# A decoder block's last PSUM banks seeded with a row, its first products split off, and a new list schedule

## The chip, the cores and the metric

The kernel runs on one core of one Trainium2 chip. The metric is the device time of one execution in microseconds. The median of 3 runs of the kernel before is 896.83 us (896.61 to 897.23).

## The reference

One layer of a decoder trunk, for one sequence of 512 positions with 1024 channels, 256 memory tokens, 4 heads, and 2816 channels in the feed-forward part, all in f32:

```python
h = rmsnorm(x, norm_mix_g)
p_a, p_b, q, p_g = split(h @ w_in)                  # 3072, 2048, 1024, 3072 columns
gb, gc, v = split(p_a)
y_a = (gb * causal_conv3(gc * v)) @ w_a_out
u, ug = split(p_b)
y_b = silu(layernorm(causal_conv31(u * sigmoid(ug)) + bias)) @ w_b_out
k, vm = split(rmsnorm(mem, norm_mem_g) @ w_kv)
y_c = attention(q, k, vm) @ w_att_out               # 4 heads, 256 memory tokens
g = sigmoid(p_g + b_gate)
x = x + (g[0] * y_a + g[1] * y_b + g[2] * y_c) @ w_o
gt, up = split(causal_conv3(rmsnorm(x, norm_ffn_g) @ w_up))
x = x + (silu(gt) * up) @ w_down
out = rmsnorm(x, norm_final_g)
```

## The kernel before

**Products.** Each f32 factor is held as a high and a low part, and each product is three matmuls: high by high, high by low, low by high (`product`, L585, whose matmuls are L589 to L591; `multiply`, L796, whose matmuls are L808 and which forms the large products from fewer block products, Strassen's way). Weights arrive in f32 in tiles `wf` of 128 x 1024 by DMA, half of them through SP's queue (L668) and half through GpSimd's (POOL, L762; these accumulate into the tile where a sum of weights is wanted). For each weight tile ScalarE casts the high part `whi` (L638) and VectorE subtracts it to get the low part `wlo` (L642); `split_job` (L615) makes these two jobs. The results of products lie in 8 PSUM banks, and VectorE and ScalarE read them from there.

**Order of the work in time.** First the keys K and values V of the memory tokens, then the input projection with the convolutions and the attention, the merge, the product with `w_o`, the product with `w_up`, whose results go through the short convolution and `silu` (L1916) and the multiplication `z` (L1899), and the product with `w_down`, in seven parts a, b, d, c, f, e, g (`pe_down`, L1997; `zl`, L2093, is the low part of its other factor).

**Who sets the order.** TensorE's work is a fixed list of jobs (`seq`). All other jobs, ScalarE's, VectorE's, GpSimd's and the loads of SP and POOL, are placed when the program is built by the class `Jobs` (L235). `latest_starts` (L280) goes back from TensorE's list to the time by which each job must start; the table `LATER` (L77) moves this due time for each kind of job, and the table `AHEAD` (L160) says how far ahead of the due time a job may start at the earliest. `run` (L354) then takes, again and again, the job that can start first, by the due time where several can. `kind` (L260) gives the name under which a job is looked up in both tables. `jobs.first` (L1945) is a list of loads with the earliest due times. So each engine has its instructions in one order that was found in this way and does not change when the program runs.

**The start.** `warm_up` (L1926) has nine dummy products. SP loads the memory tokens `mem` (L906) and the first halves of the weights of K and V (`halved_unit`, L1022, loads at L1027, cast at L1036, subtraction at L1040). `mem_high` (L910) and `mem_low` (L921) make the high and low parts `mh` (L916) and `ml` (L923) of the memory tokens. `keys_product` (L1082, matmuls at L1093) and `pe_keys` (L1128) put K's products in TensorE's list: the first block is two jobs of 12 matmuls each, and each waits for the low parts of its half. `values_product` (L1099) has V's, which use L589 to L591.

**The end.** The last part g of the product with `w_down` gives rows 256 to 511 of the left half of the output. For the last 128 rows it is computed in two PSUM banks of 256 columns each, `end_banks` (L1991), in `end_steps` (L2203), called by `steps` (L2215) and by `pe_down`. The row `x1` to which they are added lies in SBUF. `read` (L2234) adds a PSUM bank to such a row on VectorE. For the last row `read_end` (L2242) does it in three additions (L2248): first the bank that the chain of e left, then each end bank. `square` (L2250) takes the sum of squares of a part of a row on ScalarE, `half_done` (L2256) and `first_end` (L2266) combine such sums, `root` (L2271) takes the root, L2326 the reciprocal, and `right_scaled` (L2276), `left_scaled` (L2282) and `last_scaled` (L2289) scale the halves of a row and store them. The jobs are made from L2296 on. Job names: `rd` is a read, `sq` and `sr` are squares, `hd` is `half_done`, `rt` the root, `rc` the reciprocal, `sa` and `sv` the scalings of the right and the left half.

## Time and profile before

| | |
|---|---|
| median of 3 runs | 896.83 us |
| profiled execution | 897.59 us |
| its span | 895.8 us |
| TensorE (PE) busy | 885.8 us, 99% |
| VectorE (DVE) busy | 823.9 us, 92% |
| ScalarE (ACT) busy | 677.6 us, 76% |
| GpSimd (POOL) busy | 126.7 us, 14% |
| moved by DMA | 190.60 MB, mean 213 GB/s |

The profile is one execution. Its time is 1.8 us longer than its span, which begins with the first and ends with the last recorded event. Times in rows are microseconds from the start of the span. A row of the timeline has the start, the duration, the engine, the line of the kernel, the operation, what it writes and reads, how many like it follow each other, and in brackets how long the engine was idle before it and what it waited for. A weight load of TensorE (PEld) overlaps its matmuls.

### The profile page before, as it was taken

How to read it: one execution, taken by the hardware profiler on the slowest of the kernel's cores; microseconds unless marked ns; L12 is line 12 of the kernel's file. 1: busy time of each engine (PE TensorE's matmuls, PEld its weight loads, DVE VectorE, ACT ScalarE, POOL GpSimd, SP SyncE). 2: the span in 40 equal slices, each digit the busy share in tenths (PEclk: the TensorE clock that was granted, in tenths of full speed). 3: DMA queues.
4: the chain of work that ended last, by engine and by line, in shares of the span. 5: the costliest groups of instructions: out<-in, count | busy, mean ns of one | idle time of the engine just before them, and what ended most of it. 6: DMA issues, size and time to landing. Idle time of an engine off the chain costs nothing.

```text
span 895.8 us, 16734 instructions
## 1 busy us (share of the span) xinstructions
PE 885.8 (99%) x6657; PEld 848.1 (95%) x6657; DVE 823.9 (92%) x929; ACT 677.6 (76%) x934; POOL 126.7 (14%) x153
## 2 busy tenths in 40 slices
PE   9999999999999999999999999999999999999997
PEld 8999999999989999999899988899999999988886
DVE  6997999999989999999978869898998889999997
ACT  7677989988988879778948743777776677866566
POOL 0011121101011121111100001021121121002120
PEclk9999999999999999999999999999999999999999
DMA  9998788757779889987858488599999878679992
GB/s 357 386 243 181 178 205 190 178 143 164 198 158 240 170 197 223 227 210 194 210 122 273 139 252 198 147 230 308 282 259 218 205 149 167 197 266 302 251 202 94
DMA packets 54366, 190.60 MB, mean 213 GB/s; under 512 B 6160, under 2 KB 6544, under 8 KB 54288
## 3 DMA queue, kind: packets, MB, share of 16 engines
q0 software_dynamic: 20880, 75.24, 46.3%
q1 hardware_dynamic: 33120, 114.02, 36.0%
q8 instruction: 52, 0.85, 0.4%
q10 hardware_dynamic: 288, 0.27, 0.1%
q14 instruction: 26, 0.21, 0.1%
HBM read 185.31 MB, written 4.19 MB: 212 GB/s over the span
## 4 chain that ended last, share of the span: by engine, by line
PE 94%; DVE 2%; ACT 1%; issue 1%; DMA 1%; SPq 0%; DVEq 0%
PE bank L808 60%; PE bank L590 6%; PE bank L591 6%; PE bank L589 6%; PE bank L1580 5%; PE bank L1581 5%; PE bank L1582 5%; PE bank L1093 2%; DVE wlo L642 1%; DMA mem<-in_mem_t 1%; PE bank L1819 0%; PE bank L1333 0%; ACT j L2251 0%; DVE upc L1536 0%; DVE gtc L1536 0%
## 5 line engine op out<-in xcount | busy, mean ns | idle before, releaser
L638 ACT CAST whi<-wf 128x1024 fp32r<-128x1024 f32 (+1 forms) x205 | 212.2, 1040 | 72.3 <-PE bank L808 35.1
L642 DVE TENSOR_TENSOR wlo<-wf,whi 128x1024 fp32r<-128x1024 f32 (+1 forms) x199 | 239.3, 1211 | 26.4 <-ACT whi L638 26.2
L1405 ACT ACTIVATE tp<-u,pk 128x511 f32<-128x511 f32 (+22 forms) x184 | 119.7, 707 | 5.7 <-DVE acc L1412 4.0
L1412 DVE TENSOR_TENSOR acc<-acc,tp 128x1020 f32<-128x1020 f32 (+22 forms) x92 | 109.2, 1189 | 5.6 <-ACT tp L1405 3.8
L762 POOL DMA_DIRECT2D wf<-in_w_in x56 | 49.5, 899 | 255.4 <-DVE wlo L642 170.0
L808 PE MATMUL bank<-ft6h,wlo 128*128 128x256 f32 x232 | 63.9, 275 | 0.7 <-DVE wlo L642 0.7
L808 PE MATMUL bank<-fb10h,whi 128*128 128x256 f32 x232 | 64.0, 276 | 0.0
L808 PE MATMUL bank<-fb11h,whi 128*128 128x256 f32 x232 | 64.0, 276 | 0.0
L808 PE MATMUL bank<-fb00h,whi 128*128 128x256 f32 x232 | 63.9, 275 | 0.0
L808 PE MATMUL bank<-fb00l,whi 128*128 128x256 f32 x232 | 63.8, 275 | 0.0
L808 PE MATMUL bank<-fb00h,wlo 128*128 128x256 f32 x232 | 63.8, 275 | 0.0
L808 PE MATMUL bank<-fb10l,whi 128*128 128x256 f32 x232 | 63.8, 275 | 0.0
L808 PE MATMUL bank<-fb10h,wlo 128*128 128x256 f32 x232 | 63.8, 275 | 0.0
L808 PE MATMUL bank<-ft5l,whi 128*128 128x256 f32 x232 | 63.8, 275 | 0.0
L808 PE MATMUL bank<-ft5h,wlo 128*128 128x256 f32 x232 | 63.8, 275 | 0.0
L808 PE MATMUL bank<-ft6l,whi 128*128 128x256 f32 x232 | 63.8, 275 | 0.0
L808 PE MATMUL bank<-ft7l,whi 128*128 128x256 f32 x232 | 63.8, 275 | 0.0
L808 PE MATMUL bank<-ft7h,wlo 128*128 128x256 f32 x232 | 63.8, 275 | 0.0
L808 PE MATMUL bank<-ft4l,whi 128*128 128x256 f32 x232 | 63.8, 275 | 0.0
L808 PE MATMUL bank<-ft4h,wlo 128*128 128x256 f32 x232 | 63.8, 275 | 0.0
L808 PE MATMUL bank<-fb11l,whi 128*128 128x256 f32 x232 | 63.8, 275 | 0.0
L808 PE MATMUL bank<-fb11h,wlo 128*128 128x256 f32 x232 | 63.8, 275 | 0.0
(381 smaller groups left out, 3143.1 us busy)
## 6 DMA issues: line engine op xcount, KB each, us to landing
wf<-in_w_in POOLq DMA_DIRECT2D x56, 512.0 KB, 6.8
wf<-in_w_in SPq DMA_DIRECT2D x54, 512.0 KB, 5.5
wf<-in_w_up POOLq DMA_DIRECT2D x33, 512.0 KB, 7.3
wf<-in_w_up SPq DMA_DIRECT2D x29, 512.0 KB, 6.8
wf<-in_w_down SPq DMA_DIRECT2D x15, 512.0 KB, 4.5
wf<-in_w_att_out SPq DMA_DIRECT2D x8, 512.0 KB, 3.6
wf<-in_w_a_out SPq DMA_DIRECT2D x8, 512.0 KB, 3.7
wf<-in_w_b_out SPq DMA_DIRECT2D x8, 512.0 KB, 4.6
```

Of the source, the lines that this page charges most:

```text
L589: nc.tensor.matmul(ps, s_hi, w_hi, start=start, stop=False, skip_group_check=again)
L590: nc.tensor.matmul(ps, s_hi, w_lo, start=False, stop=False, skip_group_check=again)
L591: nc.tensor.matmul(ps, s_lo, w_hi, start=False, stop=stop, skip_group_check=again)
L638: nc.scalar.copy(parts[0], src())
L642: nc.vector.tensor_tensor(lo, src(), hi.bitcast(F32), op=ALU.subtract)
L762: nc.gpsimd.dma_start(out=tiles[key], in_=block(w, col[c], k), accum_op=ALU.add)
L808: nc.tensor.matmul(ps[:, c, :], w[:, i, at], in_turns(a[i]), start=first and n == 0, stop=i == 3 and n == 2, skip_group_check=again,)
L1405: nc.scalar.activation(two(("tp", p, s))[:, j, s:], two(("u", p))[:, j, : SEQ - s], AF.Copy, scale=weight(j),)
L1412: nc.vector.tensor_tensor(a, a, two(("tp", p, s))[:, :, s:], op=ALU.add)
L1580: nc.tensor.matmul(ps, w_hi[:, i, at], hi, start=first, stop=False)
L1581: nc.tensor.matmul(ps, w_hi[:, i, at], lo, start=False, stop=False)
L1582: nc.tensor.matmul(ps, w_lo[:, i, at], hi, start=False, stop=last)
```

## The change

It has three parts.

The row is put under the last product. `read_end` now writes the two end banks: each gets the sum of its 256 columns of `x1` and of the bank that the chain of e left, in two additions of 256 columns (job `rd end`). The products of part g add onto the banks (they never start them anew). The squares on ScalarE (`square_end`) and the scalings on VectorE (`last_scaled`) read the banks themselves, and the two additions after the last products are no longer there. The first of g's jobs now waits for `rd end`, the last square no longer for the scaling of row 2, and the left scaling of row 2 no longer for the last addition.

The four high-by-high matmuls of the first half of K's first block are a job `K00` that waits only for the high parts. The job after it has the other 8. On TensorE this moves three matmuls ahead of others; nothing else of its order changes.

The tables `LATER` and `AHEAD` are new: 323 entries in place of 319, and 216 in place of 195. Of the 279 kinds that `LATER` has in both, none keeps its value. `kind` now tells the rows apart for seven kinds of jobs at the end. In the built programs 481 of VectorE's lines stand differently, 424 of ScalarE's, 78 of SP's and 32 of GpSimd's. Among them: SP's first load is now V's first half, which was the seventh, and its cast and subtraction are the first of ScalarE's and VectorE's.

```diff
 LATER = {
...
-    "SP ldm": -808.23, "SP ldp": -253.98, "SP ldr": 23.82, "SP ldx": 1.04, "SP x1b": -8.53,
-    "SP xl": 30.15, "SP yl": -122.59,
...
+    "SP ld0 K": -2573.51, "SP ld0 V": -133.7, "SP ldg": -6.39, "SP ldm": -827.92, "SP ldp": -4.41,
+    "SP ldr": 93.57, "SP ldx": -4.22, "SP x1b": 5.5, "SP xl": -4.81, "SP yl": -701.62,
 }
...
-        elif key[0] in ("tap", "tp"):
+        elif key[0] in ("tap", "tp", "sa", "sv", "sq", "hd", "sr", "rt", "rc"):
             words = key[:2]
...
-    def keys_product(h, g, ks):
+    def keys_product(h, g, ks, ns=(0, 1, 2)):
         bank = ("bank", "K", h)
-        first = g == 0 and ks[0] == 0
+        first = g == 0 and ks[0] == 0 and ns[0] == 0
...
-            at, again = slice(j * P, (j + 1) * P), j > 0
+            at, again = slice(j * P, (j + 1) * P), j > 0 or ns[0] > 0
             for k in ks:
-                for n, (w, a) in enumerate(((w_hi, m_hi), (w_hi, m_lo), (w_lo, m_hi))):
+                for n in ns:
+                    w, a = ((w_hi, m_hi), (w_hi, m_lo), (w_lo, m_hi))[n]
...
         if (h, g) == (0, 0):
+            pe(("K00",), 4 * MM_QUAD, lambda: keys_product(0, 0, (0, 1), (0,)),
+               [("wh0", "K", 0), ("mh", 0, 0)], take=[(bank, "ps")], unit=False)
             for e in range(2):
-                pe(K0 if e else ("K0",), 12 * MM_QUAD,
-                   lambda e=e: keys_product(0, 0, (2 * e, 2 * e + 1)), [("wl0", "K", e), ("ml", 0, e)],
-                   take=[] if e else [(bank, "ps")], use=[bank] if e else [], unit=e == 1)
+                pe(K0 if e else ("K0",), (12 if e else 8) * MM_QUAD,
+                   lambda e=e: keys_product(
+                       0, 0, (2 * e, 2 * e + 1), (0, 1, 2) if e else (1, 2)),
+                   [("wl0", "K", e), ("ml", 0, e)], use=[bank], unit=e == 1)
...
         if p == "g":
-            banks = banks[:1] + (end_banks if u == 1 else [])
+            banks = banks[:1] + (end_banks if u < 2 else [])
+            needs += [("rd", "end")] if u == 0 else []
...
-           take=[(k, "ps") for k in (banks if new else end_banks if (p, u) == ("g", 0) else [])],
+           take=[(k, "ps") for k in (banks if new else [])],
...
-                ps = make(end_banks[i]) if k == 0 else tiles[end_banks[i]]
                 at, cols = (slice(None), k % 4, slice(P, 2 * P)), ENDS[i]
                 product(
-                    ps[:, :256], hi[:, k % 2, cols], lo[:, k % 2, cols],
+                    end_bank(i), hi[:, k % 2, cols], lo[:, k % 2, cols],
...
-                    k == 0, k == PAIRS - 1,
+                    False, k == PAIRS - 1, again=True,
                 )
...
-    def read_end(i):
-
-        row = late["x1"][NT - 1][0]
-        src = tiles["bank", chain("e"), 1]
-        if i < 2:
-            row, src = row[:, ENDS[i]], tiles[end_banks[i]][:, :256]
-        nc.vector.tensor_tensor(parted(row), parted(row), turned(src), op=ALU.add)
+    def end_bank(i):
+        return tiles[end_banks[i]][:, :256]
+
+    def read_end():
+        row, src = late["x1"][NT - 1][0], turned(tiles["bank", chain("e"), 1])
+        for i in range(2):
+            make(end_banks[i])
+            nc.vector.tensor_tensor(
+                turned(end_bank(i)), parted(row[:, ENDS[i]]), parted(src[:, i, :]), op=ALU.add)
...
+    def square_end(i, into):
+        nc.scalar.activation(late["junk"][0][:, ENDS[i]], end_bank(i), AF.Square, accum_out=into)
...
-            x1, x1, r_fin[NT - 1], late["g"][0][:, cols], op0=ALU.mult, op1=ALU.mult
+            parted(x1), turned(end_bank(i)), r_fin[NT - 1], parted(late["g"][0][:, cols]),
+            op0=ALU.mult, op1=ALU.mult,
         )
...
-                job(("rd", "end", 2), "DVE", dve(512), lambda: read_end(2),
-                    [("pd", "e", NU - 1)] + rows_in, use=[("bank", chain("e"), t)])
-                for i in range(2):
-                    job(("rd", "end", i), "DVE", dve(256), lambda i=i: read_end(i),
-                        [("pd", "g", "rest", i), ("rd", "end", 2)], use=[end_banks[i]])
+                job(("rd", "end"), "DVE", 2 * dve(256), read_end,
+                    [("pd", "e", NU - 1)] + rows_in, take=[(k, "ps=whole") for k in end_banks],
+                    use=[("bank", chain("e"), t)])
...
-            job(("sr", t, 0), "ACT", 0.4, lambda: square(last, 0, ENDS[0], ss_end),
-                [("rd", "end", 0)])
+            job(("sr", t, 0), "ACT", 0.4, lambda: square_end(0, ss_end),
+                [("pd", "g", "rest", 0)], use=[end_banks[0]])
             job("ends", "DVE", 0.1, first_end, [("sr", t, 0), ("hd", t)])
-            job(("sr", t, 1), "ACT", 0.4, lambda: square(last, 0, ENDS[1]),
-                [("rd", "end", 1), ("sa", 2)])
+            job(("sr", t, 1), "ACT", 0.4, lambda: square_end(1, ss_fin[last][:, 0:1]),
+                [("pd", "g", "rest", 1)], use=[end_banks[1]])
...
-                [("rc", t)] + ([("rd", "end", 1)] if t == 2 else []))
+                [("rc", t)])
         else:
             for i in range(2):
-                job(("sv", t, i), "DVE", 0.4, lambda i=i: last_scaled(i), [("rc", t)])
+                job(("sv", t, i), "DVE", 0.4, lambda i=i: last_scaled(i), [("rc", t)],
+                    use=[end_banks[i]])
```

90 lines of the change are left out of this document (45 added, 45 removed), and 157 rows, old and new, of tables (AHEAD, LATER).

## The prediction, made before the changed kernel was run

> **What bounds the kernel now.** I read the page first, then the waits of TensorE, then busy time by stretches of the span.
>
> ```profile
> PE 885.8 (99%) x6657; PEld 848.1 (95%) x6657; DVE 823.9 (92%) x929; ACT 677.6 (76%) x934; POOL 126.7 (14%) x153
> ```
>
> TensorE is busy for 885.8 of the span's 895.8 us, and VectorE for 92%. So there are some 10 us in which TensorE does not work, and the first question is where they lie. Below are two rows of the waits of TensorE, those for the first unit of V (in total, times, longest), and the four stretches between the first product and the end of the last (span, then busy time of PE, PEld, DVE, ACT, POOL).
>
> ```profile
> PE bank L589 <- ACT whi L1036: 0.4, 1, 0.4
> PE bank L590 <- DVE wlo L1040: 0.2, 1, 0.2
> ```
>
> ```profile
> 5.26:13.59 8.33, 7.56 (x38) 6.18 (x38) 6.17 (x11) 6.73 (x12) 0.00 (x0) 1.00 1.03 393
> 13.59:620.00 606.41, 606.41 (x4614) 582.61 (x4613) 563.52 (x626) 478.49 (x673) 82.42 (x95) 1.00 0.82 208
> 620.00:622.00 2.00, 1.31 (x12) 1.12 (x11) 2.00 (x3) 1.47 (x3) 0.00 (x0) 1.00 1.03 281
> 622.00:889.20 267.20, 266.65 (x1981) 254.27 (x1981) 249.00 (x283) 185.78 (x239) 43.53 (x50) 1.00 0.85 215
> ```
>
> Between 13.59 and 620 TensorE has no idle time at all (606.41 of 606.41). It loses 0.69 in the stretch from 620 to 622, 0.55 in the one from 622 to 889.2, 0.77 between 5.26 and 13.59, and everything before 5.26 and after 889.2. The number of products is the same in both programs, so only these five places can pay. Everything else the change moves can only cost, and only where it makes TensorE wait.
>
> **The start.** Rows of the timeline, then the loads that SP issues first, with the median time to landing last.
>
> ```profile
> 1.36 4.21 PE L1930 MATMUL bank<-ident 128*128 128x128 f32 x18 [1.36 <-POOL ident masks.py:199]
> ...
> 4.61 0.60 ACT L1036 CAST whi<-wf 128x512 fp32r<-128x512 f32 x1
> ...
> 5.26 0.58 PE L1093 MATMUL bank<-mh,whi 128*128 128x256 f32 x1
> ...
> 6.57 0.42 PE L1093 MATMUL bank<-ml,whi 128*128 128x256 f32 x1
> ...
> 6.79 0.42 PE L1093 MATMUL bank<-mh,wlo 128*128 128x256 f32 x1
> ...
> 7.70 0.28 PE L1093 MATMUL bank<-ml,whi 128*128 128x256 f32 x1
> ...
> 7.82 0.28 PE L1093 MATMUL bank<-mh,wlo 128*128 128x256 f32 x1
> ...
> 11.01 1.04 ACT L638 CAST whi<-wf 128x1024 fp32r<-128x1024 f32 x1 [0.25 <-DMA wf<-in_w_v]
> ...
> 12.27 1.22 DVE L642 TENSOR_TENSOR wlo<-wf,whi 128x1024 fp32r<-128x1024 f32 x1
> ...
> 13.59 0.38 PE L589 MATMUL bank<-whi,mh 128*128 128x512 f32 x1
> ```
>
> ```profile
> 0.75 0.38 SPq L906 DMA_DIRECT2D mem<-in_mem_t  x1
> 1.18 0.89 SPq L1027 DMA_DIRECT2D wf<-in_w_kv  x2
> ```
>
> ```profile
> wf<-in_w_kv SPq DMA_DIRECT2D x1, 256.0 KB, 3.0
> ```
>
> ```profile
> wf<-in_w_kv SPq DMA_DIRECT2D x1, 256.0 KB, 4.9
> ```
>
> The first load is issued at 0.75; the last two rows are the second, issued at 1.18, which lands 3.0 us later, and the third, issued at about 1.65, which takes 4.9. In the new program SP's first load is V's first half, so the memory tokens go from slot one to two and K's first half from two to three. ScalarE's first cast and VectorE's first subtraction are then V's.
>
> K's first half lands at 1.65 + 3.0 = 4.65 at best (as the load in slot two did) and at 1.65 + 4.9 = 6.55 at worst (as that in slot three did). From its cast to the first product it takes 5.26 − 4.61 = 0.65, so the first product comes at 5.3 to 7.2; I take 6.2, about halfway. The dummy products end at 1.36 + 4.21 = 5.57.
>
> Now the pace. Neighbouring products stand 0.22 apart at 6.57 and 0.12 apart at 7.70: TensorE works at half pace until some time between, and I take 7.4. The 7.56 busy between 5.26 and 13.59 are then 7.56 − (7.4 − 5.26) / 2 = 6.5 at full pace. Started at 6.2, 0.6 of it is done by 7.4, and the remaining 5.9 end at 13.3, where before they ended at 13.59. The 0.77 of idle time, of which 0.4 and 0.2 are the waits for V's first half (the two rows above), drops out because that half is now there first. The next unit cannot come much sooner: its load is as far back in SP's queue as before, its cast ends at 11.01 + 1.04 = 12.05 and its subtraction 1.22 later at 13.27, against 12.27 + 1.22 = 13.49 now, so 0.22 is the most that this chain gives the second product, and 0.45 the first. **Start: −0.3**, bounds −0.45 (13.14) and +0.2 (first product at 7.2: 0.1 done by 7.4, end 13.8).
>
> That the first four high-part products become a job of their own lets three of them stand ahead of the first that reads a low part. No wait separates them in these rows, so this is 0 by itself.
>
> The Trainium skill, page "TensorE: Matmul & The Clock Gate", section "What's actually happening", says that the array's clock is halved by default, released after a window of about 3.4 us of sustained work, and that these windows run freely, so that the moment differs from run to run. This trace agrees that there is such a moment, though 5.4 to 6.3 us behind the first dummy product (6.79 and 7.70 less 1.36), and the column of the granted clock, 1.00 in that stretch, does not show it. By that page the first product could meet a half pace that lasts one window longer, an estimate of +1.7 in place of −0.3.
>
> **The stall at 621.** Rows of the timeline around it, and the load's time to landing.
>
> ```profile
> 600.89 0.86 POOL L762 DMA_DIRECT2D wf<-in_w_up  x1 [0.68 <-DVE wlo L642]
> ...
> 610.15 2.02 ACT L638 CAST whi<-wf 128x1024 fp32r<-128x1024 f32 x2 [2.49 <-PE bank L808]
> 610.30 0.69 DVE L853 TENSOR_TENSOR gt<-gt,bank 128x512 f32<-128x512 f32 x1 [0.86 <-PE bank L808]
> ...
> 617.55 1.07 ACT L1916 ACTIVATE gtc<-gtc 128x1024 f32<-128x1024 f32 x1
> ...
> 619.48 1.23 DVE L1899 TENSOR_TENSOR z<-upc,gtc 128x1024 f32<-128x1024 f32 x1
> 620.62 1.22 DVE L642 TENSOR_TENSOR wlo<-wf,whi 128x1024 fp32r<-128x1024 f32 x1
> ...
> 621.89 0.38 PE L808 MATMUL bank<-ft6h,wlo 128*128 128x256 f32 x1 [0.69 <-DVE wlo L642]
> ```
>
> ```profile
> wf<-in_w_up POOLq DMA_DIRECT2D x1, 512.0 KB, 9.2
> ```
>
> The product at 621.89 waited 0.69 for a subtraction at 620.62, which stood in VectorE's queue behind z at 619.48, and VectorE had been idle 0.86 before 610.30. The cast at 610.15 is put down to a PE bank, but the load issued at 600.89 lands 9.2 later, at 610.09: that is what it waited for. In the new order the load ahead of it in GpSimd's queue has gone behind it, so this one is issued and lands earlier, and VectorE does two subtractions ahead of the addition at 610.30, in time in which it is idle now. VectorE then reaches z about 0.9 earlier, and next late is the silu on ScalarE: it ends at 617.55 + 1.07 = 618.62, then z 1.14 (to the next start, 620.62 − 619.48), then the subtraction's 1.22: 620.98. TensorE wanted it at 621.89 − 0.69 = 621.20. **Stall: −0.65** (bounds −0.69, all of it, and +0.65 if the load lands no earlier: then VectorE idles from 609.44 until the cast's first half is done at about 611.2, 1.8, where it now idles 0.86 and 0.25).
>
> **The stall at 807.** One row:
>
> ```profile
> 807.51 0.48 PE L591 MATMUL bank<-whi,zl 128*128 128x512 f32 x1 [0.38 <-DVE zl L2093]
> ```
>
> It waits for zl, which stands in both orders at the same place with equal work ahead on VectorE. **0**, bounds −0.38 (gone) and +0.38 (as much again).
>
> **The tail.** The end of the last row, before:
>
> ```profile
> 873.01 0.68 DVE L2248 TENSOR_TENSOR x<-x,bank 128x512 f32<-128x512 f32 x1
> ...
> 874.52 0.27 PE L589 MATMUL bank<-whi,zh 128*128 128x256 f32 x1
> ...
> 888.60 1.32 ACT L2278 ACTIVATE x<-x,cols 128x512 f32<-128x512 f32 x2
> ...
> 888.90 0.28 PE L591 MATMUL bank<-whi,zl 128*128 128x256 f32 x1
> ...
> 889.29 0.41 DVE L2248 TENSOR_TENSOR x<-x,bank 128x256 f32<-128x256 f32 x1
> ...
> 889.82 0.40 ACT L2251 ACTIVATE j<-x 128x256 f32<-128x256 f32 x1
> ...
> 891.39 0.97 SPq L2294 DMA_DIRECT2D out<-x  x2
> ```
>
> VectorE's addition at 889.29 goes, and the square can begin where it began: 889.82 − 889.29 = 0.53 sooner. But ScalarE's own queue holds two scalings from 888.60 that keep it until about 889.8 as well; they stand ahead of the square in the new order too. They wait for reciprocals on VectorE, and one of the dropped additions of 0.41 stood among these, so the scalings come up to 0.41 sooner. The rest of the chain (root, reciprocal, scaling, store at 891.39) is unchanged. **Tail: −0.4**, bounds −0.53 and 0 (ScalarE as late as now).
>
> The seeding costs VectorE two additions of 0.41 in place of one of 0.68, 0.14 more, and the first end product must now wait for it. Even in the old place it would end at 873.01 + 0.82 = 873.83, 0.7 before 874.52: 0. Without that cover it would cost what it is late.
>
> **The new order elsewhere** moves 481 of VectorE's lines, 424 of ScalarE's, 78 of SP's and 32 of GpSimd's, against a TensorE that does not wait. I compared for each subtraction the work ahead of it in both orders with the time until its first product. The closest are left 0.25 to 0.5 us of margin, so 0; the price if that is wrong is the last rival's.
>
> **Sum:** −0.3 − 0.65 + 0 − 0.4 = −1.35. The profiled execution took 897.59 (span 895.8 and 1.8 around it), so 896.24 for one like it. It was 0.76 above the median of the runs, 896.83, so the forecast is 895.5. About 0.2% (1.8 us) is what a measurement of this kernel can tell from no change; this lies within it.
>
> **Rivals.**
> *More goes than I count.* If the start, both stalls and the tail give their full bounds, it is −0.45 − 0.69 − 0.38 − 0.53 = −2.05, 894.8. For it: VectorE is ahead after 621. Against it: it has equal work ahead of the stall at 807.
> *Nothing is gained.* The change does not do what it says: ScalarE's scalings keep the tail, K's late landing takes back what V's early one gives, and the load at 600.89 lands no earlier. Then the terms are 0: about 896.8. For it: both ends of the tail meet at 889.8 in the rows.
> *The clock.* If K's first half lands as late as slot three did, TensorE idles from 5.57 to 7.2. If that makes it begin its half pace anew and needs as much work as the dummy products' 4.2 us, it works at half pace from 7.2 to 11.4, does 2.1 of the 6.5, and ends the rest at 15.8: +2.2 in place of −0.3, so 898.0. It decides from a landing after about 4.9, when the dummy products no longer reach the first product. Against it: the half pace lasted past 5.57 without any idle time.
> *VectorE runs dry (slower).* In the stage between 13.59 and 620 a subtraction that is moved behind others can find VectorE waiting for a cast:
>
> ```profile
> 358.78 1.22 DVE L642 TENSOR_TENSOR wlo<-('bb', 1)_553_4225,whi 128x1024 fp32r<-128x1024 f32 x1
> ...
> 365.27 0.28 PE L808 MATMUL bank<-fb10h,wlo 128*128 128x256 f32 x1
> ...
> 679.82 1.23 DVE L642 TENSOR_TENSOR wlo<-wf,whi 128x1024 fp32r<-128x1024 f32 x1 [2.05 <-ACT whi L638]
> ```
>
> The subtraction at 358.78 ends at 360.00, and its first product is at 365.27: 5.27 of slack, of which the new order, seven places later, takes about 5.0. At 679.82 VectorE did wait 2.05 for a cast. One such wait at a place with 0.25 of margin stalls TensorE 1.8; two give 895.5 + 3.6 = 899.1. It decides from a new wait of 0.25 ahead of such a place. Against it: casts and loads have mostly moved with the subtractions.
>
> **How the numbers follow.** Forecast 0.54 (895.5, from 894.8 to 896.3), more 0.11 (894.8), nothing 0.14 (896.8), the clock 0.08 (898.0), dry 0.13 (899.1). Runs of one kernel differ by ±0.3, so the range goes from 894.5 (894.8 less that) to 898.2 (898.0, with which the worst bounds agree: +0.2 + 0.65 + 0.38 + 0 gives 898.1), and leaves out the dry case and little below. Within 0.2% is 895.04 to 898.62. Faster: the case of more and a quarter of the forecast's, 0.11 + 0.14 = 0.25; slower: the dry case and 0.01 of the clock, 0.14; the same 0.61.
>
> **What would show it.** Start: V's first load in slot one, the first real product between 5.3 and 7.2, and the unit that began at 13.59 begin at about 13.3; half-pace pitch past 8 would be the clock. Stall: no wait of L808's products for a subtraction near 621, and the load that was issued at 600.89 landed before 609.5. Stall at 807: still there, 0.4. Tail: no addition between the last product and the square, and the last store's issue 2.1 instead of 2.5 us behind the start of the last product (891.39 − 888.90). Wrong if TensorE waits anywhere between 13.6 and 620, or if the span's end moves by another sum than these four.

## The result, and the profile after

The changed kernel took 900.54 us (median of 6 runs, 899.27 to 901.41) where the kernel before took 897.03 in the same series (6 runs, 896.61 to 897.48): a ratio of 1.0039, 95% interval 1.0026 to 1.0052. It is slower by 3.5 us. The forecast was 895.5, its range ended at 898.2, and the case that came true, the one on the slower side, had been given 0.13.

The profiled execution of the changed kernel took 900.1, with a span of 898.0 and 2.1 around it (before: 897.59, 895.8 and 1.8). These 0.3 outside the span are part of the loss: the six runs have 2.0 to 2.1 there, the runs of the kernel before 1.7 to 1.9. Experiments 4, 5, 9 and 10 have 2.0 to 2.3, all others 1.7 to 1.8; why is not known. Busy time of the engines on its page:

```profile
PE 886.6 (99%) x6657; PEld 847.5 (94%) x6657; DVE 823.0 (92%) x928; ACT 679.6 (76%) x934; POOL 127.0 (14%) x153
```

The work is the same to within 2 us on every engine, and VectorE has one instruction less. So the rest of the loss is waiting, and the waits of TensorE say where (in total, times, longest):

```profile
PE bank L813 <- DVE ft6l L735: 1.1, 1, 1.1
PE bank L595 <- DVE wlo L647: 0.8, 1, 0.8
PE bank L813 <- ACT bank L846: 0.7, 1, 0.7
...
PE bank L813 <- DVE wlo L647: 0.3, 1, 0.3
PE bank L594 <- DVE x L1802: 0.3, 1, 0.3
```

The first, third, fourth and fifth are new, at 601, 643, 631 and 574. Between 571 and 643 TensorE waited once before, 0.69 at 621. The second stands in the place of the wait at 807. The last three of the stretches that the prediction shows (span, then PE, PEld, DVE, ACT, POOL):

```profile
13.59:620.00 606.41, 604.89 (x4595) 580.12 (x4595) 561.59 (x625) 477.60 (x669) 82.67 (x95) 1.00 0.81 206
620.00:622.00 2.00, 2.00 (x20) 2.00 (x19) 1.72 (x2) 1.90 (x4) 0.00 (x0) 1.00 1.09 272
622.00:889.20 267.20, 265.29 (x1966) 252.63 (x1965) 247.86 (x278) 185.34 (x235) 43.59 (x50) 1.00 0.86 220
```

Before, TensorE was busy for 606.41 of the first of these; now for 604.89. The second has no idle time any more, the third has 1.91 where it had 0.55. A ledger shows it more finely: the start of the same product in both profiles, and how far the changed kernel is behind (a minus: ahead) at that point.

| place | before | after | behind | step |
|---|---|---|---|---|
| second product of V's third unit | 13.81 | 12.66 | −1.15 | −1.15 |
| first after the wait at 572 to 574 | 574.10 | 573.92 | −0.18 | +0.97 |
| first that reads ft6l, at 599 to 601 | 599.49 | 601.02 | +1.53 | +1.71 |
| after the old stall | 621.89 | 622.75 | +0.86 | −0.67 |
| after the wait at 631 | 630.04 | 631.35 | +1.32 | +0.46 |
| after the wait at 643 | 640.53 | 642.84 | +2.30 | +0.98 |
| one at 700 | 700.05 | 702.60 | +2.55 | +0.25 |
| last product | 888.90 | 891.72 | +2.81 | +0.26 |
| end of the span | 895.8 | 898.0 | +2.2 | −0.6 |

So the start gave more than was forecast, the tail too, and four places in the new order between 555 and 645 took back 4.1 (0.97 + 1.71 + 0.46 + 0.98 + 0.25, the last of these right behind 643, less 0.24 of the first step that was lost before 530). With the old stall's 0.67 that is 3.5 lost in this stretch.

**The largest step, 599 to 601.** The timeline of the kernel before, GpSimd, ScalarE and VectorE, sorted by time:

```profile
580.40 0.86 POOL L762 DMA_DIRECT2D wf<-in_w_up  x1 [6.58 <-ACT whi L638]
587.01 0.86 POOL L762 DMA_DIRECT2D wf<-in_w_up  x1 [5.74 <-ACT h2b L1844]
...
593.25 2.01 ACT L638 CAST whi<-wf 128x1024 fp32r<-128x1024 f32 x2
593.70 1.22 DVE L595 SCALAR_TENSOR_TENSOR h2b<-h2b,h2b 128x1024 f32<-128x1024 f32 x1
594.83 2.35 DVE L642 TENSOR_TENSOR wlo<-wf,whi 128x1024 fp32r<-128x1024 f32 x2
597.10 1.22 DVE L730 TENSOR_TENSOR ft6l<-h2b,ft6h 128x1024 fp32r<-128x1024 f32 x1
```

And of the changed kernel:

```profile
584.56 0.86 POOL L767 DMA_DIRECT2D wf<-in_w_up  x1 [8.16 <-DVE cols L1819]
587.09 1.76 POOL L767 DMA_DIRECT2D wf<-in_w_up  x2 [1.66 <-ACT h2b L1853]
...
594.64 1.06 ACT L643 CAST whi<-wf 128x1024 fp32r<-128x1024 f32 x1 [2.27 <-DMA wf<-in_w_up]
...
595.74 1.23 DVE L647 TENSOR_TENSOR wlo<-wf,whi 128x1024 fp32r<-128x1024 f32 x1 [1.99 <-ACT whi L643]
596.88 1.22 DVE L600 SCALAR_TENSOR_TENSOR h2b<-h2b,h2b 128x1024 f32<-128x1024 f32 x1
...
599.15 0.68 DVE L1846 TENSOR_TENSOR fb11l<-bank,fb11h 128x512 fp32r<-128x512 f32 x1
599.75 1.22 DVE L735 TENSOR_TENSOR ft6l<-h2b,ft6h 128x1024 fp32r<-128x1024 f32 x1
...
601.02 0.38 PE L813 MATMUL bank<-ft6l,whi 128*128 128x256 f32 x1 [1.08 <-DVE ft6l L735]
```

The load issued at 587.09 (before: 587.01) is the same one. The time to its landing, after and before:

```profile
wf<-in_w_up POOLq DMA_DIRECT2D x1, 512.0 KB, 7.5
```

```profile
wf<-in_w_up POOLq DMA_DIRECT2D x1, 512.0 KB, 5.6
```

The reader is to see a chain of three queues. Issued at the same time, the load lands 1.9 later; on GpSimd's queue another went out 2.5 ahead of it (584.56) and not 6.6 (580.40), and experiment 5 below tries this cause. ScalarE stands 2.27 before the cast. VectorE stands 1.99 before the subtraction that needs the cast, and **behind this subtraction in VectorE's queue is the addition to h2b, whose input has long been there**. Before, the addition stood ahead, at 593.70; now it starts at 596.88, and ft6l, which needs it, comes 2.65 later (599.75 against 597.10). The load is not the whole of this: 1.99 are the idle time, and 0.60 are fb11l (599.15), which the new order puts ahead of ft6l (before: 600.51, behind it). TensorE used up what lead it had and waited 1.08.

**The same pattern at 630**, and, with one of the loads of in_w_o, at 560. At 643 it is ScalarE's queue: a copy of a bank, which came at 638.05 before, stands at 642.21 behind a cast that waited 1.12 for its load.

```profile
559.23 2.00 ACT L643 CAST whi<-wo 128x1024 fp32r<-128x1024 f32 x2 [3.55 <-DMA wo<-in_w_o]
560.31 1.22 DVE L647 TENSOR_TENSOR wlo<-wo,whi 128x1024 fp32r<-128x1024 f32 x1 [2.30 <-ACT whi L643]
...
628.99 1.05 ACT L643 CAST whi<-('up', 3)_943_7121 128x1024 fp32r<-128x1024 f32 x1 [2.30 <-DMA ('up', 3)_943_7121<-in_w_up]
630.07 1.23 DVE L647 TENSOR_TENSOR wlo<-('up', 3)_943_7121,whi 128x1024 fp32r<-128x1024 f32 x1 [2.44 <-ACT whi L643]
```

One line of VectorE's waits between 590 and 645 sums up its part, before and after: waiting for casts of weights rose from 2.6 to 6.5.

```profile
DVE wlo L642 <- ACT whi L638: 2.6, 5, 0.9
```

```profile
DVE wlo L647 <- ACT whi L643: 6.5, 6, 2.4
```

**The old stall at 621** is gone, but not by the forecast's reason. The forecast's load, which was to land before 609.5, lands when its cast starts; z starts 0.8 later than before (620.28 against 619.48), not 0.9 sooner. TensorE was itself 1.5 late by then, so it no longer stood there first:

```profile
610.06 1.05 ACT L643 CAST whi<-wf 128x1024 fp32r<-128x1024 f32 x1 [0.83 <-DMA wf<-in_w_up]
...
620.28 1.23 DVE L1908 TENSOR_TENSOR z<-upc,gtc 128x1024 f32<-128x1024 f32 x1 [0.35 <-DMA wf<-in_w_up]
```

**The wait at 807** became one of 0.8 at 807.18, for a subtraction that VectorE does at the end of a row without a break; TensorE catches up with VectorE there. **The tail**: the square reads the bank, 0.31 after the last product starts, and the last store is issued 893.58 − 891.72 = 1.86 after it, where it was 2.49.

```profile
891.72 0.28 PE L596 MATMUL bank<-whi,zl 128*128 128x256 f32 x1
...
892.03 0.39 ACT L2268 ACTIVATE j<-bank 128x256 f32<-128x256 f32 x1 [0.26 <-PE bank L596]
...
893.58 1.02 SPq L2309 DMA_DIRECT2D out<-x  x2
```

### The profile page after: what moved, and what is told of

Its sections match the earlier page's. It is cut to its first block, busy times and chain, and to the rows that moved or that the text cites. A ratio compares the mean times of both kernels' runs of the same rounds, so it can differ in the third digit from the quotient of the medians.

```text
span 898.0 us, 16745 instructions
## 1 busy us (share of the span) xinstructions
PE 886.6 (99%) x6657; PEld 847.5 (94%) x6657; DVE 823.0 (92%) x928; ACT 679.6 (76%) x934; POOL 127.0 (14%) x153
## 4 chain that ended last, share of the span: by engine, by line
PE 90%; DMA 5%; DVE 2%; issue 1%; ACT 1%; SPq 0%; DVEq 0%; ACTq 0%
PE bank L813 56%; PE bank L596 6%; PE bank L594 6%; PE bank L595 6%; PE bank L1589 5%; PE bank L1590 5%; PE bank L1591 5%; DMA ('up', 3)_943_7121<-in_w_up 3%; PE bank L1099 2%; DMA wo<-in_w_o 1%; DVE wlo L647 1%; DMA wf<-in_w_kv 0%; ACT whi L643 0%; PE bank L1342 0%; PE bank L1828 0%
## 5 line engine op out<-in xcount | busy, mean ns | idle before, releaser
L643 ACT CAST whi<-wf 128x1024 fp32r<-128x1024 f32 x202 | 209.9, 1043 | 83.3 <-PE bank L813 34.9
L647 DVE TENSOR_TENSOR wlo<-wf,whi 128x1024 fp32r<-128x1024 f32 x196 | 236.0, 1213 | 29.5 <-ACT whi L643 29.0
L1421 DVE TENSOR_TENSOR acc<-acc,tp 128x1018 f32<-128x1018 f32 (+22 forms) x92 | 109.1, 1190 | 9.1 <-ACT tp L1414 7.2
L767 POOL DMA_DIRECT2D wf<-in_w_in x53 | 46.7, 908 | 240.4 <-DVE wlo L647 124.0
L813 PE MATMUL bank<-ft6h,whi 128*128 128x256 f32 x232 | 64.0, 276 | 0.1
L813 PE MATMUL bank<-ft4h,whi 128*128 128x256 f32 x232 | 63.9, 275 | 0.0
```

The lines of the kernel that those rows point to most:

```text
L643: nc.scalar.copy(parts[0], src())
L647: nc.vector.tensor_tensor(lo, src(), hi.bitcast(F32), op=ALU.subtract)
L767: nc.gpsimd.dma_start(out=tiles[key], in_=block(w, col[c], k), accum_op=ALU.add)
L813: nc.tensor.matmul(ps[:, c, :], w[:, i, at], in_turns(a[i]), start=first and n == 0, stop=i == 3 and n == 2, skip_group_check=again,)
L1421: nc.vector.tensor_tensor(a, a, two(("tp", p, s))[:, :, s:], op=ALU.add)
```

## The experiments

Theories at the outset, after the result. **Theory 1**: the new places of work between 530 and 650 make VectorE stand still behind casts whose loads are late; the start and the tail are worth what the profile says. **Theory 2**: the lead that the new start gives cannot be kept, whatever the order, because loads and engines further on do not follow; the middle only takes back what was given. Theories 3 and 4 make 1 more exact. **Theory 3**: within theory 1, it is the place of single loads on GpSimd's queue. **Theory 4**: the tail's gain is in the new order at the end, not in the bank that is seeded.

All experiments keep the changed kernel's code, with its seeded banks and its job K00. The list schedule is worked out with the old and the new tables side by side. `MIX` picks the jobs that take their place and due time from the new schedule, by their start in it (`at`, us by the planner's own clock) and their engine; all others take them from the old one. `MOVES` moves single jobs within the queue of their engine. The `before` of each ratio is the kernel before, run on the same chip in the same series.

**1. The old order.** Both tables and the kinds of jobs as before; only the code changes.

```diff
-        elif key[0] in ("tap", "tp", "sa", "sv", "sq", "hd", "sr", "rt", "rc"):
+        elif key[0] in ("tap", "tp"):
...
-LATER, AHEAD of the change
+LATER, AHEAD of the kernel before
```

> The changed kernel's code (row under the last product, first block split) with the tables of before, so that everything else keeps the order of before. Theory 1 (the loss lies in the new order of the work between 570 and 645 us and at 804 us, the other two parts of the change are worth what the tail of the changed profile shows, 0.6): 0.6 below the kernel before, about 896.4. Rival (the seeded banks are held longer and cost TensorE a wait earlier): 897.0 or above, with a new wait of TensorE before 875.

Measured: 897.04 (11 runs, 896.38 to 898.26), ratio 1.0001 [0.9992, 1.0009]. The span after the last product's start is 6.9, as before. So the banks that hold the row, and K00, are worth nothing that 11 runs can show in the old order (the interval is ±0.8), where 0.6 less had been expected, and the 3.5 us are the new order's.

**2. The new start alone.**

```diff
-MIX = None
+MIX = lambda at, e, k: at < 16.0
```

> As the run with the old order, but each job that the new schedule starts in its first 16 us stands as in the new schedule. Theory 1 (the start is a gain by itself and is kept): 1.15 below the run with the old order, about 895.3, and the product that came at 571.93 in the kernel before comes at about 570.8. Theory 2 (TensorE is then ahead of loads that land no sooner, so that the lead is spent in waits for them between 570 and 645): about 896.4, with waits of TensorE in that stretch that the run with the old order does not have.

Measured: 897.02 (11 runs, 895.98 to 897.88), ratio 0.9997 [0.9988, 1.0006]. The lead at V's third unit is 0.85 and at the last product 0.64: it is kept for 870 us. Theory 2 falls, and so does theory 1's 895.3. The time of its runs doesn't gain from it against experiment 1, which had a lead of 0.59 with the old start; see below. The tail is 6.9, as with the old order, and the stall at 621 is there with 0.7.

**3. The new middle alone.**

```diff
+MIX = lambda at, e, k: 530.0 <= at < 650.0
```

> As the run with the old order, but each job that the new schedule starts between 530 and 650 us stands as in the new schedule; the start is the old one, so TensorE has no lead. Theory 1 (the order in this stretch costs what TensorE loses there in the changed profile, 1.0 + 1.7 - 0.7 + 0.5 + 1.0 = 3.5): 3.5 above the run with the old order, about 899.9. Theory 2 (the waits come from the lead of 1.15): without the lead they shrink by about that much, so about 898.7 or less.

Measured: 903.05 (5 runs, 902.85 to 903.7), ratio 1.0066 [1.0053, 1.0079]. With no new start there is hardly a lead to take back (0.52), and the loss is all the larger: 1.16 behind by 549, 3.67 by 574, 4.77 by 599, 5.04 by 640. Theory 2 falls again. The loss is above theory 1's, because the seam at 530 adds waits of its own at 549 and 571: this run shows the place, not the size.

**4. One subtraction moved.** In the changed kernel, the subtraction that needs the late load goes behind the addition to h2b, and its cast behind the next job of ScalarE; the loads stay where they are.

```diff
+MOVES = [(("wl", (("up", 0), 6)), "behind", ("h2", "t6")),
+         (("wh", (("up", 0), 6)), "behind", ("r1", ("up", 1)))]
```

> The changed kernel with two jobs moved: the cast of one weight tile stands on ScalarE behind the two copies that now follow it, and its subtraction on VectorE behind the addition that now waits behind it. In the changed profile VectorE idles 1.99 before this subtraction at 595.74, and TensorE then waits 1.1 at 601.02. Theory 1a (that wait comes from the place of this one subtraction ahead of a load that lands late): the wait at 601 goes, 1.7 less than the changed kernel, about 898.8. Rival 1b (VectorE is short of work that is ready, whatever stands first; the idle time only moves to the next subtraction): 900.0 to 900.5, with another wait of TensorE between 595 and 625.

Measured: 898.88 (11 runs, 897.47 to 901.13), ratio 1.0019 [1.001, 1.0028], 1.7 below the changed kernel. The profile, of the longest of these runs (901.13), still has the stall: the load, with the same one 2.5 ahead of it as in the changed kernel, took 9.4 to land and not 7.5, the cast waits 3.10 for it, and TensorE waits 0.9 twice. Behind these two waits TensorE works at half pace from 601.8 to 605.0 (products 0.21 apart and not 0.11, granted clock 0.56 between 602 and 605.5), which costs 1.6 more. The median speaks for the place in VectorE's queue, the trace for the load; the run does not decide it.

**5. The load moved.** The same load ahead of its neighbour on GpSimd's queue, nothing else.

```diff
+MOVES = [(("s6", ("up", 0)), "ahead of", ("s7", ("up", 1)))]
```

> The changed kernel with one load moved: on GpSimd's queue the load that the cast at 594.64 waits for (issued at 587.09 in the changed profile, 7.5 to landing) stands ahead of the one issued at 584.56. Nothing moves on the other engines. Theory 3 (the wait of 1.1 at 601 comes from this load landing 2 us later than the schedule reckoned, because it is issued behind another): the cast does not wait, the stall at 601 goes, 1.7 less than the changed kernel, about 898.8. Rival (VectorE is late there whatever lands first): the stall of 1.1 stays, about 900.5.

Measured: 898.27 (11 runs, 897.42 to 899.96), ratio 1.0017 [1.0008, 1.0026], 2.3 below the changed kernel. One load changes its place with its neighbour, and the stall at 599 to 601 is gone. GpSimd and ScalarE in this run, and the load's time to landing:

```profile
587.41 2.64 POOL L821 DMA_DIRECT2D wf<-in_w_up  x3 [10.69 <-ACT h2b L1907]
...
593.26 1.05 ACT L697 CAST whi<-wf 128x1024 fp32r<-128x1024 f32 x1 [0.56 <-DMA wf<-in_w_up]
```

```profile
wf<-in_w_up POOLq DMA_DIRECT2D x1, 512.0 KB, 5.8
```

Issued 0.3 later than in the changed kernel (587.41, first of three), it lands 1.7 sooner after its issue, and its cast starts at 593.26 in place of 594.64. At the first product that reads ft6l the kernel is 0.29 behind, not 1.53, and the wait at 643 has gone too.

**6. The old middle from 585 on.**

```diff
+MIX = lambda at, e, k: not 585.0 <= at < 645.0
```

> The changed kernel, but each job that the old schedule starts between 585 and 645 us, and that the new one does too, stands as in the old schedule, loads included. Theory 1 (the order in this stretch costs 1.7 - 0.7 + 0.5 + 1.0 = 2.5): 2.5 less than the changed kernel, about 898.0, with the stall of 0.7 at 621 back. Rival (VectorE comes into the stretch late, by what lies before 585, and loses the same whatever its order there): 900.0 or above.

Measured: 900.7 (5 runs, 899.16 to 901.08), ratio 1.0036 [1.0023, 1.0048]: no gain, against 898.0 expected. The bounds were badly put. The load that goes out ahead of the late one was issued at 584.14, so it kept its new place, and the cast still came at 594.65 after a wait of 1.72 for its load. But the old order has the addition to h2b ahead of the subtraction (593.25), no product waits for ft6l, and TensorE loses 0.3 at 599, not 1.7. What the run loses instead, 2.2 between 602 and 645, it loses behind that, with a new wait of 1.5 for ScalarE at 621. So the late load alone is not the stall at 599 to 601: what stands behind its subtraction belongs to it.

**7. The new start and everything from 650 on.**

```diff
+MIX = lambda at, e, k: at < 16.0 or at >= 650.0
```

> As the run with the new start and the old order, but from 650 us on each job stands as in the new schedule. Theory 1 (behind 650 the new order costs 1.2 - 0.7 = 0.5 at 804 to 808 and gives 0.6 in the tail): within 0.2 of the run with the new start, about 897.0; TensorE waits about 0.8 at 804. Rival (the wait at 804 comes from the lateness brought along from before 650): no wait at 804, 0.6 less than the run with the new start, about 896.4.

Measured: 897.3 (11 runs, 896.08 to 898.24), ratio 1.0001 [0.9992, 1.0009]. All of the change but the stretch from 16 to 650 is not measurably slower than before; that stretch is worth 3.4 (1.0039 less 1.0001, of 897), the 0.3 outside the span among it.

**8. The new start and the new tail.**

```diff
+MIX = lambda at, e, k: at < 16.0 or at >= 870.0
```

> As the run with the new start and the old order, but from 870 us on each job stands as in the new schedule: only the start, the seeded row and the order of the last 25 us are new. Theory 4 (seeding the row gives nothing as long as the two scalings on ScalarE end as late as before; with the new order of the tail it gives 0.6): the span ends 6.3 instead of 6.9 behind the start of the last product, 0.6 less than the run with the new start, about 896.4. Rival (the 0.6 of the changed profile is scatter of the last stores): 6.9, about 897.0.

Measured: 896.15 (11 runs, 895.27 to 897.74), ratio 0.999 [0.9981, 0.9999]. It is the only version whose whole interval lies below the kernel before, by 0.9 in the middle, and it is 4.4 below the changed kernel. The ratios put the stretch from 650 to 870 at some 1.0 (0.9990 against 1.0001), though their intervals overlap. The two profiles show 0.25 of it at 804 to 808; most of the rest, 0.5, lies between 610 and 625, where all engines have the same order in both and experiment 7's cast at 607.30 waited 2.13 for its load, experiment 8's 0.61. ScalarE and SP at the end, first in experiment 2 (old order, last product at 888.26), then in this one (new order, last product at 888.55):

```profile
887.21 1.94 ACT L2475 ACTIVATE x<-x,cols 128x512 f32<-128x512 f32 x3
...
889.05 0.36 ACT L2451 ACTIVATE j<-bank 128x256 f32<-128x256 f32 x1
...
890.58 1.10 SPq L2492 DMA_DIRECT2D out<-x  x2
```

```profile
887.26 1.33 ACT L2475 ACTIVATE x<-x,cols 128x512 f32<-128x512 f32 x2
...
888.87 0.38 ACT L2451 ACTIVATE j<-bank 128x256 f32<-128x256 f32 x1 [0.28 <-PE bank L779]
```

In the old order three scalings stand ahead of the square and keep ScalarE until it starts, 0.79 after the last product; in the new one there are two, ScalarE waits 0.28 for the bank, and the square starts 0.32 after the product. The store follows at +2.32 and at +1.86. Theory 4 holds: without the new order there, ScalarE's scalings hide the whole gain of the seeded banks (6.9 left after the last product's start in experiments 1 and 2), with it the tail is 6.3.

**9. A subtraction at 804.** Experiment 5, and the subtraction for which TensorE waits at 807 ahead of a multiply-add.

```diff
+MOVES = [(("s6", ("up", 0)), "ahead of", ("s7", ("up", 1))),
+         (("wl", ("pd", "b", 2)), "ahead of", (("cf", 10, 0), 0, 1))]
```

> The changed kernel with the load moved ahead as in the run before, and on VectorE the subtraction that TensorE waits for at 803.7 ahead of the four multiply-adds, where the old order has it. Theory 5 (the late part at 804 to 808 is set by VectorE, which is busy without a break from about 755 on and reaches the last z as late as before; the wait at 803.7 is only the first place where this shows): the wait of 0.8 at 804 goes, the wait for the low part of z at 807 takes its place, and the time stays within 0.2 of the run with the load moved, 898.3. Rival (the place of this one subtraction is the cost): 0.6 less, about 897.7.

Measured: 899.54 (11 runs, 898.2 to 900.55), ratio 1.0023 [1.0014, 1.0032]. In its profile the wait of 0.8 has gone, and one of 0.4 for zl, as in the kernel before, has come in its place. The median is 1.3 above experiment 5, which nothing in its profile explains, and the intervals of the two ratios overlap: that stays open.

**10. Two additions at 560.** Experiment 5, and the additions to x ahead of the subtraction that stood 2.30 idle at 560.

```diff
+MOVES = [(("s6", ("up", 0)), "ahead of", ("s7", ("up", 1))),
+         (("x1", "c", 0), "ahead of", ("wl", ("wo", "e", 0))),
+         (("x1", "c", 1), "ahead of", ("wl", ("wo", "e", 0)))]
```

> The changed kernel with the load moved ahead, and on VectorE two additions to the rows (which the changed profile has at 561.45) ahead of the subtraction at 560.31, before which VectorE idles 2.30 for a cast that waits for a load. Theory 3 (TensorE loses its lead at 571 to 574 because VectorE stands idle there with work that is ready behind the idle time): VectorE comes to the normalisation before 571 by 0.7 to 1.2 sooner, TensorE keeps 0.8 of its lead, about 897.5. Rival (VectorE is held there by something else, the additions' own banks or the sums of squares on ScalarE): within 0.2 of the run with the load moved, 898.3.

Measured: 899.64 (7 runs, 898.82 to 901.59), ratio 1.0029 [1.0018, 1.004]. The loss at 571 to 574 stays, 0.7. The additions now wait themselves, 1.55 and 0.60, for banks of TensorE, and the casts of in_w_o still wait 3.23 for their load. At this place the order of these additions is not the cause. The profiles of the versions that have the same order of loads there say what is: where that pair of casts starts at 558.81 to 559.55 (the changed kernel, experiments 5, 6 and 10), TensorE loses 0.5 to 0.7 at 571 to 574; where it starts at 557.49 and 557.61 (experiments 9 and 4), nothing. So it is the landing of in_w_o, and that differs from execution to execution.

**11. The load one place later, in the good version.** Experiment 8, and the load of experiment 5 behind its neighbour.

```diff
+MIX = lambda at, e, k: at < 16.0 or at >= 870.0
+MOVES = [(("s6", ("up", 0)), "behind", ("s5", ("up", 1)))]
```

> The best version so far (new start, old order, new tail) with one load moved the other way: on GpSimd's queue the load that the run with the load moved brought forward stands one place later, behind the next one. Nothing moves on the other engines. Theory 3 (a load that lands about 2 to 3 us later at this place costs TensorE 1.7 in any order): a wait of TensorE of 0.8 to 1.5 at 599 to 602 and about 1.5 more than without the move, 897.6. Rival (the old order of VectorE and ScalarE has the slack for it): within 0.3 of 896.15, no such wait.

Measured: 903.56 (5 runs, 902.65 to 903.92), ratio 1.0069 [1.0057, 1.0082], 7.4 above experiment 8. One load, one place:

```profile
587.76 2.64 POOL L950 DMA_DIRECT2D wf<-in_w_up  x3 [7.85 <-PE bank L2011]
...
598.31 1.99 ACT L826 CAST whi<-wf 128x1024 fp32r<-128x1024 f32 x2 [6.30 <-DMA wf<-in_w_up]
...
601.30 0.38 PE L996 MATMUL bank<-ft6h,whi 128*128 128x256 f32 x1 [3.11 <-ACT ft6h L914]
...
602.94 0.58 PE L996 MATMUL bank<-ft6l,whi 128*128 128x256 f32 x1 [1.26 <-DVE ft6l L918]
```

```profile
603.00:609.00 6.00, 6.00 (x29) 6.00 (x29) 5.08 (x6) 1.37 (x3) 0.86 (x1) 0.51 0.98 218
```

Second of three issued without a pause, it lands 9.9 after its issue and is cast at 598.31. ScalarE stands 6.30 and TensorE 3.11 + 1.26. The direction and the chain are theory 3's; the size is five times what was expected, for two reasons. The load lands 6.0 later than in experiment 8, not 2 to 3. And behind the two waits TensorE works at half pace: its products are 0.21 apart until 608.9, and the row above, for 603 to 609, shows 29 products in 6 us and a granted clock of 0.51 (last but two). That costs 2.9 of the 7.4. All five runs have a mean granted clock of 0.994 to 0.996, experiment 8's have 0.998 to 1.

**12. The old start with the new tail.**

```diff
+MIX = lambda at, e, k: at >= 870.0
```

> The best version so far without the new start: the old order up to 870 us and the new one behind it. If the new start is worth what the profiles show at 14 us (the second product of the third unit of V comes 0.92 before that of the profile before on the mean of seven profiles with the new start, 0.37 on the mean of three with the old one), 0.5 above 896.15, about 896.7; if the start is worth nothing, 896.15. The tail is 6.3 in either case.

Measured: 896.65 (11 runs, 895.64 to 898.61), ratio 0.9998 [0.9989, 1.0007]: 0.5 above experiment 8, within the scatter of both. The tail is 6.3. Its profile has a lead of 1.04 at V's third unit **with the old start**, as large as the new start's.

By then it was open whether late loads alone, or the moved casts and subtractions alone, make the loss. Two runs take one without the other, each on top of experiment 8.

**13. The new loads, the old engines.**

```diff
+MIX = lambda at, e, k: (at < 16.0 or at >= 870.0
+                        or 570.0 <= at < 645.0 and e not in ("DVE", "ACT"))
```

> The best version (new start, old order, new tail, 896.15), but the loads that the new schedule starts between 570 and 645 us (on both queues) stand as in the new schedule; VectorE's and ScalarE's jobs keep the old order. Theory 3 (the order of the loads is the cost): 1.5 to 4 more, 897.7 to 900, and ScalarE's casts wait for loads between 590 and 605. Theory 1 (the order of the work on the two engines is the cost): within 0.5 of 896.15.

Measured: 897.78 (12 runs, 896.42 to 900.34), ratio 1.0005 [0.9997, 1.0014], 1.6 above experiment 8. The cast of 594.84 waits 1.43 for its load, but the addition to h2b stands ahead of the subtraction there, and no product waits for ft6l. Its profile loses 0.7 between 570 and 645, where experiment 8's loses 0.3, and 0.9 at 651 to 657, behind the stretch that was exchanged.

**14. The old loads, the new engines.**

```diff
+MIX = lambda at, e, k: (at < 16.0 or at >= 870.0
+                        or 570.0 <= at < 645.0 and e in ("DVE", "ACT"))
```

> The best version (896.15), but VectorE's and ScalarE's jobs that the new schedule starts between 570 and 645 us stand as in the new schedule; the loads keep the old order. Theory 3: within 0.7 of 896.15, since the loads land as before. Theory 1: 1.5 to 3 more, 897.7 to 899.

Measured: 899.1 (7 runs, 899.05 to 900.66), ratio 1.0025 [1.0014, 1.0035], 2.95 above experiment 8. VectorE's waits for casts between 590 and 645, in experiments 8, 13 and 14:

```profile
DVE wlo L830 <- ACT whi L826: 1.9, 4, 0.9
```

```profile
DVE wlo L830 <- ACT whi L826: 4.3, 6, 1.0
```

```profile
DVE wlo L830 <- ACT whi L826: 6.0, 6, 1.3
```

The order on the two engines is the larger half. With the new loads VectorE stands 4.3 and the kernel loses 1.6; with the new order on the engines 6.0 and 2.95, as theory 1 had it; with both, in the changed kernel, 6.5 (experiment 7's ratio puts the whole stretch from 16 to 650 at 3.4). In the profiles experiment 14 loses 2.95 between 570 and 645, the changed kernel 3.5. Theory 3, which allowed 0.7 with the old loads, is wrong as a theory of the whole loss. At 599 to 601 it takes both halves: with the load late and the addition behind its subtraction (the changed kernel) TensorE waits 1.08 for ft6l; with the load as late and the addition ahead (experiments 6 and 13), or with the addition behind and the load early (experiment 5), it does not wait for it. So what decides there is whether the order of the casts matches the order in which their loads land, and what stands behind a cast that doesn't; for the other places this is read from the traces only.

## Why the prediction was wrong, step by step

**The start, −0.3.** Right in sign. This pair of profiles shows −1.15, outside its bounds, but about half of that is the start of the profile of before, not the change. With the new start, the twelve profiles stand 0.19 to 1.46 ahead of that profile at V's third unit, 0.9 in the mean; with the old start it is 0, 0.52, 0.59 and 1.04, 0.54 in the mean. The difference, 0.4, agrees with the term, though with this scatter that is partly luck, and the medians give 0 (experiments 1 and 2) to 0.5 (8 and 12). The chain that was to allow 0.45 at most is not the limit: even with the old start one profile (experiment 12) is 1.04 ahead. V's load is in slot one, and the first real product comes at 5.91, between the 5.3 and 7.2 that were given:

```profile
0.75 0.39 SPq L1032 DMA_DIRECT2D wf<-in_w_v  x1
```

```profile
5.91 0.71 PE L1099 MATMUL bank<-mh,whi 128*128 128x256 f32 x4 [0.34 <-ACT whi L1041]
...
6.85 0.28 PE L1099 MATMUL bank<-ml,whi 128*128 128x256 f32 x1
6.96 0.28 PE L1099 MATMUL bank<-mh,wlo 128*128 128x256 f32 x1
```

**The clock rival, 898.0.** Not here: the pitch is 0.11 by 6.85, although TensorE did idle 0.34 before the first product. It came elsewhere. At the start, in experiment 13, the half pace lasts longer: neighbouring products stand 0.21 apart until 9.98. And in the middle of the kernel it does begin anew behind idle time, as the rival supposed: in experiment 11 (2.9 lost) and in the profile of experiment 4 (1.6). Of the changed kernel's six runs the two longest, 901.24 and 901.41, have a mean granted clock of 0.996 and the others 0.998 or more, so it may be in these two; no trace shows it. The rows of experiment 13:

```profile
9.77 0.42 PE L1282 MATMUL bank<-ml,whi 128*128 128x256 f32 x1
9.98 0.32 PE L1282 MATMUL bank<-mh,wlo 128*128 128x256 f32 x1
```

The Trainium skill's statement that was weighed there (page "TensorE: Matmul & The Clock Gate", section "What's actually happening"), that the windows of the clock run freely and the moment differs from run to run, agrees: full pace, a pitch of 0.11 in place of 0.21, is seen from 4.99 in experiment 1 (still in the dummy products), from 6.24 in the changed kernel, from 7.70 in the kernel before and from 10.25 in experiment 13, with the first dummy product at 1.36 in all four. That fits the small lead of experiment 13 (0.19); that it is the main reason for the scatter of the start is not shown, since experiment 12 came to full pace later than experiment 1 (6.07) and has the larger lead.

**K00, 0, and the seeding, 0.** Nothing against it: experiment 1, 1.0001 ± 0.0008.

**The stall at 621, −0.65.** The mechanism was wrong. The load issued around 601 did not land earlier, and VectorE came to z later, not sooner. The wait went because TensorE was behind. In experiment 2, with the same start and the old order, it is there; in experiment 5, which lost less before, 0.8 of it is there with the new order.

**The stall at 807, 0.** Wrong by 0.3 in the profile (2.55 behind at 700, 2.81 at the end), as a new wait of 0.78 where one of 0.38 was, within the bound of +0.38; experiments 5 and 7 show the same 0.3. "Equal work ahead" was true of zl; it was not asked how early the subtraction before it could be.

**The tail, −0.4.** Right in sign and nearly in size (−0.6, beyond the bound of −0.53), but by luck. The forecast let the scalings come up to 0.41 sooner because an addition drops out; experiment 1 has just that, and its tail is no shorter than before (6.9). That ScalarE's scalings could hide the gain was seen; that the new order takes one of three scalings out from in front of the square was not, and it is what frees the gain (experiment 8).

**The new order elsewhere, 0.** This is the step that failed: "I compared for each subtraction the work ahead of it in both orders with the time until its first product." It is worth +4.1 in the profile, +3.5 with the old stall's end, and +3.4 in experiment 7's ratio. The comparison counted VectorE's work only. It did not ask when the cast comes that the subtraction needs, nor when the load lands that the cast needs, nor what stands behind the subtraction. The margins of 0.25 to 0.5 were taken as safe; the cast at 594.64 alone waited 2.27 where it had not waited at all.

**The rival "VectorE runs dry".** It had the mechanism (a moved subtraction waits for a cast, with needed work behind), the price per place (a wait of 2.05 was taken; 1.99, 2.30 and 2.44 came), the number of places (two; four came, of which one large) and nearly the time, 899.1 for 900.54. What it lacked was that the casts wait for late loads, and its chance of 0.13 was far too low. What was held against it, that "casts and loads have mostly moved with the subtractions", is what was wrong: they moved, and the load whose neighbour on GpSimd's queue had moved to 2.5 ahead of it landed 1.9 later.

Shown by runs: that the loss is the order's between 16 and 650 (1, 7, 8); that most of it comes with the order on VectorE and ScalarE between 570 and 645 (14); that the place of one load there is worth 2.3 (5) and up to 7.4 (11, of which 2.9 are half pace); that at 599 to 601 late load and place on VectorE's queue must come together (changed kernel, 5, 6, 13). Only read from the trace: the causes at 571 to 574, 630 and 643. Open: the 0.3 outside the span, and why experiment 9 took longer than 5.

## What to carry to other kernels

Where a new order moves work against an engine that never waits, check three times for each moved operation: when its load lands, when the cast in front of it ends, and what is queued behind it on its own engine; equal work ahead is not enough. Leave room for a load to land some 2 us later than in the one profile that was read. Read a load's landing from its issue and from what was issued shortly ahead of it on the same queue, and put on an in-order queue nothing urgent behind an operation whose input may be late. A shorter chain at the end pays only if the engine that it goes through is free by then: look for what stands in its queue.

## What the runs showed of the hardware

Loads of 512 KB on GpSimd's queue around 587 took, from issue to landing: with one issued 2.5 ahead 7.5 (changed kernel), 7.9 (experiment 6) and 9.4 (experiment 4); as the second of three without a pause 9.4 (experiment 5) and 9.9 (experiment 11); with no other issued for 6.6 or more ahead 5.6 (before), 5.8 (experiment 5) and 5.5 (experiment 11). But the load at 580.40 in the kernel before, with none for 7.4 ahead of it, took 7.4, so the place on this queue is not all that counts. The Trainium skill, page "DMA: Bandwidth & Descriptors", section "Queues, rings and completion order", says that each DMA engine takes turns between the queues it has work for, a packet at a time. No run here shows whether transfers on other queues made the 7.4 at 580.40 so long; that loads issued shortly ahead on its own queue go with a later landing is shown by the times above only.

TensorE's half pace can come back in the middle of a kernel: in experiment 11 behind waits of 3.11 and 1.26, in experiment 4 behind two of 0.89 that lie 0.4 apart. In the changed kernel's profile the wait of 1.08 brought none.

The landing of a load differs between executions of one order. In the profiles of experiments 5 and 9, which have the same order there, one pair of casts of in_w_o starts 2.06 apart, and TensorE loses 0.6 at 571 to 574 in the first and nothing in the second:

```profile
559.55 1.99 ACT L697 CAST whi<-wo 128x1024 fp32r<-128x1024 f32 x2 [3.40 <-DMA wo<-in_w_o]
```

```profile
557.49 1.99 ACT L697 CAST whi<-wo 128x1024 fp32r<-128x1024 f32 x2 [1.68 <-DMA wo<-in_w_o]
```
